# Attention with given scores: the loads of a pass's last two heads moved into a branch, the very last ones in small pieces

## The chip, the cores and the metric

One core of one Trainium2 chip. The metric is the device time of one execution in microseconds (us), the median of several runs.

## The reference

```python
scores: (8, 12, 1024, 1024) float32      v: (8, 12, 1024, 64) float32

def reference(scores, v):
    scores_max = np.max(scores, axis=-1, keepdims=True)
    attn = np.exp(scores - scores_max)
    attn = attn / (np.sum(attn, axis=-1, keepdims=True) + 1e-8)
    return np.matmul(attn, v).astype(np.float32)
```

There are 96 heads (8 x 12). Each has 4 MB of scores, 0.25 MB of v and 0.25 MB of results.

## The kernel before

A loop runs 24 passes of four heads (`AHEAD = 4`). For each head, ScalarE takes the exponential of the scores, two of eight rows at a time (a "row" here is one 128 x 1024 tile), TensorE transposes the tile in eight blocks, VectorE copies the transposed tile from PSUM, and TensorE multiplies it with v, to which a column of ones is joined so that the row sums come out with the product. GpSimd casts v to 16 bits (`vones`) beforehand. The products of a row are emitted two rows later (`LAG = 2`).

```python
    def load(k, n, step=R, **cond):
        queue(nc.sync.dma_start(out=v_bufs[k][:], in_=one(v_bh, n), **cond))
        for r in range(0, R, step):
            queue(nc.sync.dma_start(out=s_bufs[k][:, r : r + step, :],
                                    in_=one(sc_bh, n)[:, r : r + step, :], **cond))

    def load_next(k, n0):
        n = (n0 + (AHEAD + k)) % BH
        load(k, n, R if k < AHEAD - 1 else R // 2, cond=n0 < BH - AHEAD)

    def heads(n0):
        for k in range(AHEAD):
            nc.gpsimd.tensor_copy(out=vones_bufs[k][:, :, 0:D], in_=v_bufs[k][:])
            ...
            for r in range(R):
                if r % EB == 0:
                    p_nat = take(p_bufs)
                    nc.scalar.activation(out=p_nat[:], in_=s_bufs[k][:, r : r + EB, :], func=EXP)
                ...                       # 8 transposes, copy to pt
                if r == R - 1:
                    load_next(k, n0)      # the same buffer, for the next pass
                pending.append((n0 + k, r, pt, st))
                if len(pending) > LAG:
                    finish(pending.pop(0))   # products, division, store of a head
        while pending:
            finish(pending.pop(0))
```

All loads and stores are issued by the sync engine, in order. The framework gives each transfer one of eight completion semaphores in turn; I call them lanes 0 to 7. A transfer's issue waits until the lane's previous user has landed, and whoever reads the data waits for a count on that lane. The packed trace of this kernel has both: the second half of head 95 landed at 1057.22 us and the issue that waited for it began at 1057.35; the scores of head 94 landed at 1046.24 and the exp that waited for them began at 1046.34.

The softmax here doesn't subtract the row's maximum and nothing guards it: scores larger than these inputs give would overflow.

## Time and profile before

| | |
|---|---|
| time | 1071.87 us (1071.53 to 1072.08) |
| span of the profile | 1070.1 us |
| bytes moved | 453.05 MB, at 423 GB/s on average |
| busy: TensorE, ScalarE, VectorE | 70%, 69%, 57% |
| last scores land (read from the sync engine's waits) | about 1057.3 us |
| last exp ends, last result is ready, span ends | 1061.05, 1066.29, 1070.1 us |

Read it from the transfers: their rate is level until the last slice, so the only part of the time that is not transfer is what follows the last byte, some 13 us.

### The profile page before, as it was taken

How to read it: one execution, taken by the hardware profiler on the slowest of the kernel's cores; microseconds unless marked ns; L12 is line 12 of the kernel's file. 1: busy time of each engine (PE TensorE's matmuls, PEld its weight loads, DVE VectorE, ACT ScalarE, POOL GpSimd, SP SyncE). 2: the span in 40 equal slices, each digit the busy share in tenths (PEclk: the TensorE clock that was granted, in tenths of full speed). 3: DMA queues.
4: the chain of work that ended last, by engine and by line, in shares of the span. 5: the costliest groups of instructions: out<-in, count | busy, mean ns of one | idle time of the engine just before them, and what ended most of it. 6: DMA issues, size and time to landing. Idle time of an engine off the chain costs nothing.

```text
span 1070.1 us, 31933 instructions
## 1 busy us (share of the span) xinstructions
PE 752.8 (70%) x12288; PEld 711.3 (66%) x12288; DVE 610.7 (57%) x1157; ACT 733.8 (69%) x408; POOL 60.1 (6%) x102
## 2 busy tenths in 40 slices
PE   3766768677676776677766768668676776767766
PEld 3766767577666676576765758567675676666766
DVE  2655656456565565555655656556564565655655
ACT  4767766677667776676856767677666776576865
POOL 0000000000000000000000000000000000000000
PEclk9888888778897888877887888888897788878889
DMA  9999999999999999999999999999999999999995
GB/s 401 430 410 430 430 431 425 432 436 431 431 426 425 434 427 425 431 431 430 433 427 434 420 442 430 421 433 426 429 426 434 432 431 431 429 424 440 430 420 228
DMA packets 44787, 453.05 MB, mean 423 GB/s; under 512 B 4976, under 2 KB 4976, under 8 KB 29552
## 3 DMA queue, kind: packets, MB, share of 16 engines
q1 hardware_dynamic: 44784, 453.00, 99.7%
q8 instruction: 3, 0.05, 0.0%
HBM read 445.64 MB, written 25.17 MB: 440 GB/s over the span
## 4 chain that ended last, share of the span: by engine, by line
DMA 67%; PEld 9%; PE 9%; DVE 5%; ACT 5%; SPq 2%; issue 2%; ACTq 0%
DMA s_nat<-in_scores_dram 67%; PEld L169 7%; PE psT L169 6%; DVE pt L175 5%; ACT p_nat L163 5%; PE psO L105 3%; PEld L105 3%; SPq L140 1%; SPq L143 1%; SPq L124 0%; DVE recip L116 0%; ACTq L163 0%; DVE out_sb L117 0%
## 5 line engine op out<-in xcount | busy, mean ns | idle before, releaser
L163 ACT ACTIVATE p_nat<-s_nat 128x2048 f16<-128x2048 f32 x384 | 703.0, 1902 | 159.2 <-DMA s_nat<-in_scores_dram 157.0
L175 DVE COPY pt<-psT 128x1024 f16<-128x1024 f16 x768 | 516.3, 690 | 432.3 <-PE L169 214.5
L169 PE MATMUL psT<-ident,p_nat 128*128 128x128 f16 x6144 | 569.7, 251 | 267.3 <-ACT p_nat L163 266.6
L169 PEld LDWEIGHTS <-p_nat 128*128 128x128 f16 x6144 | 492.9, 153 | 282.2 <-ACT p_nat L163 277.7
L105 PE MATMUL psO<-vones,pt 128*128 128x65 f16 x6144 | 374.8, 205 | 45.3 <-DVE pt L175 38.9
L105 PEld LDWEIGHTS <-pt 128*128 128x128 f16 x6144 | 305.2, 106 | 71.8 <-DVE pt L175 70.1
L163 ACT ACT_TABLE_LOAD x24 | 30.8, 1283 | 168.1 <-DMA s_nat<-in_scores_dram 163.2
L158 POOL CAST vones<-v_sb 128x512 f16<-128x512 f32 x96 | 59.4, 619 | 987.6 <-DMA v_sb<-in_v_dram 725.0
L117 DVE TENSOR_TENSOR out_sb<-psO,recip 128x256 f32<-128x256 f32 x192 | 81.1, 422 | 4.9
L116 DVE RECIPROCAL recip<-psO 128x4 f32<-128x4 f32 x192 | 33.5, 174 | 17.2 <-PE psO L105 17.2
L57 DVE MEMSET vones<- 128x8 f16 x4 | 0.2, 65 | 0.8 <-PEq L204 0.8
L51 DVE CAST ident<-ident 128x128 f16<-128x128 f32 x1 | 0.2, 226 | 0.3 <-POOL ident masks.py:199 0.3
masks.py:199 POOL TENSOR_SCALAR_AFFINE_SELECT ident<-ident 128x128 f32<-128x128 f32 x1 | 0.3, 294 | 0.1
masks.py:197 POOL MEMSET ident<- 128x128 f32 x1 | 0.2, 205 | 0.3 <-POOLq L204 0.3
L204 POOL MEMSET const-float32-0.0<- 128x1 f32 x1 | 0.1, 99 | 0.2 <-issue 0.2
L204 POOL MEMSET const-bfloat16-1.0<- 128x1 bf16 x1 | 0.1, 102 | 0.0
L204 POOL MEMSET const-uint8-127<- 128x1 uint8 x1 | 0.1, 102 | 0.0
L204 POOL MEMSET const-float32-1.0<- 128x1 f32 x1 | 0.1, 99 | 0.0
## 6 DMA issues: line engine op xcount, KB each, us to landing
s_nat<-in_scores_dram SPq DMA_DIRECT2D x76, 4096.0 KB, 27.1
s_nat<-in_scores_dram SPq DMA_DIRECT2D x48, 2048.0 KB
v_sb<-in_v_dram SPq DMA_DIRECT2D x100, 256.0 KB, 17.2
out_dram<-out_sb SPq DMA_DIRECT2D x96, 256.0 KB, 21.1
```

What stands on the lines that cost most here:

```text
L51: nc.vector.tensor_copy(out=ident16[:], in_=ident32[:])
L57: nc.vector.memset(vo[:, :, D : D + 1], 1.0)
L105: nc.tensor.matmul(out=psO[:, g, :], lhsT=pt[:, c * P : (c + 1) * P], rhs=st["vones"][:, c, :], start=(c == 0), stop=(c == C - 1),)
L116: nc.vector.reciprocal(out=recip[:], in_=psO[:, :, D : D + 1])
L117: nc.vector.tensor_tensor(out=st["out_sb"][:, r - G + 1 : r + 1, :], in0=psO[:, :, 0:D], in1=recip[:].to_broadcast([P, G, D]), op=mybir.Al ...
L140: queue(nc.sync.dma_start(out=v_bufs[k][:], in_=one(v_bh, n), **cond))
L143: nc.sync.dma_start(out=s_bufs[k][:, r : r + step, :], in_=one(sc_bh, n)[:, r : r + step, :], **cond,)
L158: nc.gpsimd.tensor_copy(out=vones_bufs[k][:, :, 0:D], in_=v_bufs[k][:])
L163: nc.scalar.activation(out=p_nat[:], in_=s_bufs[k][:, r : r + EB, :], func=EXP)
L169: nc.tensor.transpose(out=psT[:, c * P : (c + 1) * P], in_=p_row[:, c, :], identity=ident16[:],)
L175: nc.vector.tensor_copy(out=pt[:], in_=psT[:])
L204: nc = _bacc.Bacc("TRN2", target_bir_lowering=False, num_devices=1)
```

## The change

The intent is to shorten that tail. If the last head arrives in small pieces, ScalarE and TensorE can be nearly done when the last row lands. Small pieces are wanted for the last two heads alone, and in a loop that takes a branch. The branch stands at the end of the pass, so the loads of a pass's heads 2 and 3 (k = 2, 3) are issued after all else of the pass.

```diff
-    def load(k, n, step=R, **cond):
+    def load(k, n, parts=(R,), **cond):
         queue(nc.sync.dma_start(out=v_bufs[k][:], in_=one(v_bh, n), **cond))
-        for r in range(0, R, step):
+        r = 0
+        for rows in parts:
 ...
     def load_next(k, n0):
-        n = (n0 + (AHEAD + k)) % BH
-        load(k, n, R if k < AHEAD - 1 else R // 2, cond=n0 < BH - AHEAD)
+        if k < AHEAD - 2:
+            load(k, (n0 + (AHEAD + k)) % BH, cond=n0 < BH - AHEAD)
+
+    def load_last(n0):
+        ks = range(AHEAD - 2, AHEAD)
+        before = queued[-1:]
+        with tc.If(n0 == BH - 2 * AHEAD) as cmp:
+            queued[:] = before
+            for k, parts in zip(ks, ((4, 4), (2, 2, 2, 1, 1))):
+                load(k, (n0 + (AHEAD + k)) % BH, parts)
+        with cmp.Else():
+            queued[:] = before
+            for k in ks:
+                load(k, (n0 + (AHEAD + k)) % BH, cond=n0 < BH - AHEAD)
 ...
-                    nc.scalar.activation(out=p_nat[:], in_=s_bufs[k][:, r : r + EB, :], func=EXP)
+                    rows = 1 if k == AHEAD - 1 and r == R - EB else EB
+                    for g in range(0, EB, rows):
+                        nc.scalar.activation(out=p_nat[:, g : g + rows, :],
+                                             in_=s_bufs[k][:, r + g : r + g + rows, :], func=EXP)
 ...
         while pending:
             finish(pending.pop(0))
+        load_last(n0)
```

More of the change, by code (lines that the diff above doesn't have):

```diff
@@ L137, in apart @@
         )
-    def load(k, n, step=R, **cond):
+    def load(k, n, parts=(R,), **cond):
         queue(nc.sync.dma_start(out=v_bufs[k][:], in_=one(v_bh, n), **cond))
-        for r in range(0, R, step):
+        r = 0
+        for rows in parts:
             queue(
                 nc.sync.dma_start(
-                    out=s_bufs[k][:, r : r + step, :],
-                    in_=one(sc_bh, n)[:, r : r + step, :],
+                    out=s_bufs[k][:, r : r + rows, :],
+                    in_=one(sc_bh, n)[:, r : r + rows, :],
                     **cond,
@@ L148, in load @@
             )
+            r += rows
     def load_next(k, n0):
-        n = (n0 + (AHEAD + k)) % BH
-        load(k, n, R if k < AHEAD - 1 else R // 2, cond=n0 < BH - AHEAD)
+        if k < AHEAD - 2:
[11 more added lines that the diff above has]
+                load(k, (n0 + (AHEAD + k)) % BH, cond=n0 < BH - AHEAD)
     def heads(n0):
@@ L162, in heads @@
                     p_nat = take(p_bufs)
-                    nc.scalar.activation(
-                        out=p_nat[:], in_=s_bufs[k][:, r : r + EB, :], func=EXP
-                    )
+                    rows = 1 if k == AHEAD - 1 and r == R - EB else EB
+                    for g in range(0, EB, rows):
+                        nc.scalar.activation(
+                            out=p_nat[:, g : g + rows, :],
+                            in_=s_bufs[k][:, r + g : r + g + rows, :],
+                            func=EXP,
+                        )
                 p_row = p_nat[:, r % EB, :].rearrange("p (q c) -> p c q", c=C)
```

## The prediction

> **What bounds the kernel now.** I read the page first, for the load of the DMA queue and the chain that ended last.
>
> ```profile
> GB/s 401 430 410 430 430 431 425 432 436 431 431 426 425 434 427 425 431 431 430 433 427 434 420 442 430 421 433 426 429 426 434 432 431 431 429 424 440 430 420 228
> DMA packets 44787, 453.05 MB, mean 423 GB/s; under 512 B 4976, under 2 KB 4976, under 8 KB 29552
> ...
> DMA 67%; PEld 9%; PE 9%; DVE 5%; ACT 5%; SPq 2%; issue 2%; ACTq 0%
> ```
>
> The transfer rate is flat at about 430 GB/s in all slices but the last: the scores come in as fast as the queue moves them, and no engine is over 70% busy. Only the last slice, 26.75 us, has slack (228 GB/s). So a gain can come only from there, unless the change makes the queue run dry in the middle, which would lose time. Second, the sync engine's timeline over the second-last pass and part of the last.
>
> ```profile
> 1003.12 0.34 SPq L140 DMA_DIRECT2D v_sb<-in_v_dram  x1
> 1004.00 0.33 SPq L143 DMA_DIRECT2D s_nat<-in_scores_dram  x1
> ...
> 1013.43 0.33 SPq L140 DMA_DIRECT2D v_sb<-in_v_dram  x1
> ...
> 1015.75 0.33 SPq L140 DMA_DIRECT2D v_sb<-in_v_dram  x1
> ...
> 1024.48 0.33 SPq L140 DMA_DIRECT2D v_sb<-in_v_dram  x1
> 1025.36 1.19 SPq L143 DMA_DIRECT2D s_nat<-in_scores_dram  x2
> ...
> 1035.43 0.36 SPq L124 DMA_DIRECT2D out_dram<-out_sb  x1
> ...
> 1057.35 0.07 SPq L140 DMA_DIRECT2D v_sb<-in_v_dram  x1
> ```
>
> Each load and store uses one of eight completion semaphores in turn ("lanes" below; the built program's list of waits shows which), and an issue waits until the lane's previous user has landed. So these times are also landing times: 1013.4 is when the last head of a pass has landed (91), 1024.4 head 92, 1035.4 head 93, 1057.3 the second half of head 95. Heads land 11.0 us apart. At 1013.4 one whole load (head 92, issued 1004.0) stands in the queue, and that keeps it full. Third, the tail, by engine.
>
> ```profile
> 983.75 2.88 PE L169 MATMUL psT<-ident,p_nat 128*128 128x128 f16 x24 [6.37 <-ACT p_nat L163]
> ...
> 988.60 0.69 PE L169 MATMUL psT<-ident,p_nat 128*128 128x128 f16 x8
> ...
> 989.38 0.69 PE L169 MATMUL psT<-ident,p_nat 128*128 128x128 f16 x8
> ...
> 1036.68 0.62 POOL L158 CAST vones<-v_sb 128x512 f16<-128x512 f32 x1 [10.36 <-DMA v_sb<-in_v_dram]
> ...
> 1046.34 14.71 ACT L163 ACTIVATE p_nat<-s_nat 128x2048 f16<-128x2048 f32 x8 [3.60 <-DMA s_nat<-in_scores_dram]
> ...
> 1065.87 0.42 DVE L117 TENSOR_TENSOR out_sb<-psO,recip 128x256 f32<-128x256 f32 x1
> 1066.32 0.36 SPq L124 DMA_DIRECT2D out_dram<-out_sb  x1
> ```
>
> GpSimd's cast at 1036.68 is that of v of head 94, whose load stands ahead of that head's scores. The scores of head 94 land whole at 1046.24. ScalarE then runs the eight exps of heads 94 and 95 without a pause to 1061.05, 3.8 us after the last data. The last result is ready at 1066.29, its store goes at 1066.32, the span ends at 1070.1. That tail is what the change aims at.
>
> [...] here 24 transposes take 2.88 us after 6.37 us of idleness (120 ns each) and 8 take 0.69 us later. [...]
>
> **The change part by part.**
>
> Steady state. The loads of the pass's heads 2 and 3 now come after the store of head 3, so after everything else of the pass. Let head 3 land at 0. Its four exps take 7.3 us (8 ran in 14.71), and results come some 5 us after the last exp (1061.05 to 1066.29), so store and branch are reached at about 13. Heads 0 and 1 of the next pass, issued by 0 as before, land at 11 and 22. The queue has some 9 us of work left when head 2's load is issued. The lanes' waits in the normal branch (head 0 landed before head 2's load; head 1 landed, at 22, before the branch is left) leave enough too: head 2's load runs from 22 to 33 with head 3's behind it. No gap: 0 us. The branches [...] and one more exp a pass (about 0.1 us) lie beside transfers: 0 us.
>
> End of the data. The same bytes, except that the store of head 91 now stands ahead of the last loads: 0.26 MB at 430 GB/s is 0.6 us. The last row lands at 1057.3 + 0.6 = 1057.9.
>
> Tail as meant. Half of head 94 lands at about 1042, so ScalarE is no longer behind: the last single-row exp (about 0.97, half of 1.90 and a little) ends at 1058.9.
>
> Tail as built. The two branches use the lanes differently, and one wait must hold for both. In the normal branch lane 0 is first advanced by an empty increment, then by v of head 2: v is the lane's third user of the pass. In the last-heads branch v of head 94 is the second and the last single row of head 95 the third. GpSimd's cast of v for head 2 waits for the full three (the built program's wait value is the pass's last count of this lane). So the cast for head 94, at 1036.68 before, must wait for the very last row: 1057.9 + 0.1, and 0.62 for itself, is 1058.6. TensorE goes in order and lags by two rows: it transposes rows 0, 1 and 2 of head 94, then stands at the first product with v. From 1058.6 it has 13 transposed rows and 16 product rows left, with all exps done. Cold, one row of both takes 1.29 us (transposes started at 1039.31 and 1040.60, at a granted clock of 0.50), warm 0.79 by the starts at 988.60 and 989.38; VectorE needs 0.645 for a copy in a run and (0.17 + 0.42)/4 for the division, 0.80, so I take 0.80. First 3.4 us cold: 2.6 rows. The other 10.4 x 0.80 = 8.3. The last two products behind the copy: 1.2. Sum 1058.6 + 3.4 + 8.3 + 1.2 = 1071.5, and 0.65 for reciprocal and division: 1072.15, against 1066.29: **+5.9 us**.
>
> End. In the last pass the branch's four loads are skipped after the last store, at 0.6 us each (skipped v to skipped s: 1059.29 to 1059.88)[...]. **+0.9 us**. Sum: 1071.84 + 5.9 + 0.9 = **1078.6 us**.
>
> **The rivals.** (a) The tail as meant, the wait on the lane being looser than I read it: from the last exp at 1058.9, transposes 0.6, copy 0.7, products 0.45, reciprocal and division 0.65: 1061.3, so -5.0, and +0.9: 1067.7 us. For it speaks the change's intent; against it the wait value, which is the same register value in every pass and has to be right for the normal branch. (b) The queue runs dry once a pass, because heads 2 and 3 are asked for a head later: against it 9 us of queued work; if head 3's compute took 23 instead of 13 us, it would lose a microsecond or more in each of 23 passes, 1100 us or more. [...] (c) The wait stands, but TensorE with a full backlog keeps the pace of ScalarE-fed pairs in the tail before, 1.93 us for two rows: 10.4 x 0.165 = 1.7 us more, 1080.3. (d) [...] the cold stretch is a second window long: 1 to 2 us more.
>
> **Range and chances.** The spread of (c) and (d) above the value[...] make 1074.5 to 1083. Reading (a) has 7%, (b) 4%. The 2% limits are 1050.4 and 1093.3: neither tail reaches them; only (b) passes the upper. Faster 0.01, same 0.95, slower 0.04.
>
> **What would show it.** GpSimd's second-last cast (v of head 94) starting beside the last one, near 1058, after a wait of some 30 us, would show the lane; so would TensorE idle from about 1046 to 1058 and then 13 us of solid work, with ScalarE done by 1059. Rates of 430 GB/s in the slices before, and landings 11.0 us apart, would show the steady state untouched. Stores of the last pass all after 1058. I am wrong if that cast starts near 1037, or if slices in the middle fall under 420 throughout.

Passages of the recorded text that no trace of this case showed are cut where marked, and with them terms of its sum. For the end it had 3.3 us behind the last result, against 2.4 before, hence the +0.9.

Two of its figures can be read from traces. The first is the 3.4 us that TensorE runs cold, at a granted clock of 0.50. In the trace before, the clock is 0.50 from 1038.51 to 1041.92 and from 1048.75 to 1052.16, 3.41 us each, and for 3.56 us from the first of the 24 transposes at 983.75. But the packed trace has longer stretches as well: of 58 at half clock, 25 last 3.41 us, 24 last 6.83 and 9 last 10.24. So the "second window" of rival (d) is to be read as one more 3.4 us at half clock, worth 1.3 us by the figures of the prediction (3.4 less 2.6 rows of 0.80); its "1 to 2" is an estimate. The second is the exp more in a pass: in the trace after, five exps take 7.41 us (at 1013.56) where four take 7.33, so 0.08 us.

## The result, and the profile after

| | before | after |
|---|---|---|
| time, median | 1071.87 us | 1082.47 us (1082.28 to 1082.69) |
| ratio | | 1.0099 (95% interval 1.0082 to 1.0117) |
| span of the profile | 1070.1 us | 1080.7 us |

A ratio here and below is the mean time of one kernel's runs over the mean of the other's in the same rounds, so not quite the ratio of the medians. The change costs 10.6 us.

First the page of the changed kernel: the rates of 40 slices (27.0 us each now), and the totals.

```profile
GB/s 397 426 427 425 430 432 435 424 425 435 428 434 427 437 427 431 427 431 430 432 427 423 433 428 438 425 437 427 437 422 433 432 428 428 423 436 425 441 415 53
DMA packets 42195, 453.05 MB, mean 419 GB/s; under 512 B 4688, under 2 KB 4688, under 8 KB 29520
...
DMA 4%; issue 1%; PEld 1%; PE 1%; DVE 1%; SPq 0%; ACT 0%; DVEq 0%; ACTq 0%
```

The rate in the middle is what it was; the last slice falls from 228 to 53 GB/s. The same bytes move at the same pace, and afterwards there is more time in which nothing moves. The chain of waits, which led back to the start before, 67% of it transfers, now covers only what follows 982.5 us, and it books TensorE's standstill in the tail as 11.0 us of "issue", which is to say without a cause. So the timelines have to tell it. Next the sync engine's timeline over the second-last pass and the start of the last (columns: start, length, line, operation; x3 merges three issues with the waits between them).

```profile
1003.26 0.33 SPq L144 DMA_DIRECT2D s_nat<-in_scores_dram  x1
...
1013.51 0.33 SPq L140 DMA_DIRECT2D v_sb<-in_v_dram  x1
...
1014.95 11.10 SPq L124 DMA_DIRECT2D out_dram<-out_sb  x3
1026.55 0.35 SPq L140 DMA_DIRECT2D v_sb<-in_v_dram  x1
1027.26 1.22 SPq L144 DMA_DIRECT2D s_nat<-in_scores_dram  x2
...
1034.83 3.20 SPq L144 DMA_DIRECT2D s_nat<-in_scores_dram  x5
1057.57 0.10 SPq L140 DMA_DIRECT2D v_sb<-in_v_dram  x1
```

Head 91 has landed at 1013.5 as before. The branch is entered at 1026.5, 13 us later; the five pieces of head 95 follow when head 93 has landed (1034.8, before 1035.4). The skipped load at 1057.57 waits for the last row: the data end at 1057.5, against 1057.3 before. Now the tail by engine.

```profile
1057.59 1.18 POOL L173 CAST vones<-v_sb 128x512 f16<-128x512 f32 x2 [31.82 <-DMA s_nat<-in_scores_dram]
```

```profile
1042.29 3.71 ACT L180 ACTIVATE p_nat<-s_nat 128x2048 f16<-128x2048 f32 x2 [0.16 <-DMA s_nat<-in_scores_dram]
...
1055.07 3.80 ACT L180 ACTIVATE p_nat<-s_nat 128x2048 f16<-128x2048 f32 x3 [0.54 <-DMA s_nat<-in_scores_dram]
```

```profile
1046.58 0.42 PE L105 MATMUL psO<-vones,pt 128*128 128x65 f16 x8
1058.26 0.55 PE L105 MATMUL psO<-vones,pt 128*128 128x65 f16 x7 [11.26 <-POOL vones L173]
...
1065.61 0.68 PE L188 MATMUL psT<-ident,p_nat 128*128 128x128 f16 x8
...
1071.57 0.68 PE L188 MATMUL psT<-ident,p_nat 128*128 128x128 f16 x8
```

```profile
1074.44 0.42 DVE L117 TENSOR_TENSOR out_sb<-psO,recip 128x256 f32<-128x256 f32 x1
1074.89 0.33 SPq L124 DMA_DIRECT2D out_dram<-out_sb  x1
1076.19 0.10 SPq L140 DMA_DIRECT2D v_sb<-in_v_dram  x1
...
1077.77 0.07 SPq L144 DMA_DIRECT2D s_nat<-in_scores_dram  x1
```

The casts of v of heads 94 and 95 run together at 1057.59, and the bracket says what ended GpSimd's 31.82 us of idleness: a transfer of *scores*. A cast of v has no use for scores. The one for head 94 ran at 1036.68 before. ScalarE does what the change intended: it starts head 94 at 1042.29 instead of 1046.34 and ends at 1058.87, 1.4 us after the last byte. But TensorE stands still for 11.3 us for the cast, and all the rest of heads 94 and 95 comes after it. The clock and the busy time in the two stretches that follow:

```profile
1058.00:1064.00 6.00, 5.75 (x74) 5.74 (x74) 2.86 (x5) 0.87 (x1) 0.76 (x2) 0.50 0.23 87
1064.00:1075.00 11.00, 8.89 (x169) 8.15 (x167) 8.45 (x17) 0.00 (x0) 0.00 (x0) 1.00 0.06 24
```

The columns are the stretch, its length, busy time of PE, PEld, DVE, ACT and POOL, then TensorE's granted clock, the share of the transfer engines and GB/s. TensorE is busy almost throughout the first 6 us, but at half clock.

### The profile page after: what moved, and what is told of

The parts are those of the page before. It is cut to its first block, busy times and chain, and to the rows that moved or that the text cites. A ratio compares the mean times of both kernels' runs of the same rounds, so it can differ in the third digit from the quotient of the medians.

```text
span 1080.7 us, 32380 instructions
## 1 busy us (share of the span) xinstructions
PE 765.6 (71%) x12288; PEld 726.4 (67%) x12288; DVE 610.0 (56%) x1157; ACT 736.2 (68%) x432; POOL 59.8 (6%) x102
## 5 line engine op out<-in xcount | busy, mean ns | idle before, releaser
L180 ACT ACTIVATE p_nat<-s_nat 128x2048 f16<-128x2048 f32 (+1 forms) x408 | 705.4, 1800 | 253.0 <-DMA s_nat<-in_scores_dram 130.6
L188 PE MATMUL psT<-ident,p_nat 128*128 128x128 f16 x6144 | 586.7, 255 | 256.2 <-ACT p_nat L180 255.4
L188 PEld LDWEIGHTS <-p_nat 128*128 128x128 f16 x6144 | 503.6, 154 | 273.7 <-ACT p_nat L180 270.3
L105 PEld LDWEIGHTS <-pt 128*128 128x128 f16 x6144 | 310.9, 107 | 73.7 <-DVE pt L194 59.2
```

Of the source, the lines that this page charges most:

```text
L105: nc.tensor.matmul(out=psO[:, g, :], lhsT=pt[:, c * P : (c + 1) * P], rhs=st["vones"][:, c, :], start=(c == 0), stop=(c == C - 1),)
L180: nc.scalar.activation(out=p_nat[:, g : g + rows, :], in_=s_bufs[k][:, r + g : r + g + rows, :], func=EXP,)
L188: nc.tensor.transpose(out=psT[:, c * P : (c + 1) * P], in_=p_row[:, c, :], identity=ident16[:],)
```

## The experiments

The theory: in both arms of the branch, transfers use the lanes in turn, but nine in one arm and four in the other, so the normal arm is filled up with empty increments (additions to a semaphore without a transfer, so that both arms leave it at the same count). On lane 0 the pass's first user is v of head 0; then come the increment and v of head 2 in the normal arm, but v of head 94 and the last row of head 95 in the other. One wait value serves both, and it is the later one. The packed trace of the changed kernel bears this out, in records that the views of `prof` do not print. In the normal arm the sync engine adds to lane 0's semaphore at 982.48 and then issues v of head 2 on it at 982.96. In the other arm v of head 94 lands on lane 0 at 1037.32 and the last row on the same lane at 1057.44; GpSimd's wait on that semaphore ends at 1057.46. The rival: the branch, the late issue or the small pieces cost the time by themselves. Each experiment was run in three rounds. The fifth answers what the third left open.

**1. Eight transfers instead of nine.** The last head in four pieces, so that no lane is used twice in the arm.

```diff
-            for k, parts in zip(ks, ((4, 4), (2, 2, 2, 1, 1))):
+            for k, parts in zip(ks, ((4, 4), (2, 2, 2, 2))):
```

> The changed kernel with the last head in pieces of 2,2,2,2 rows, so that the last-heads branch issues eight transfers and none shares its completion lane with v of head 94. Lane theory: GpSimd's cast of v of head 94 starts near 1037 instead of 1057.6, TensorE does not idle for 11 us, the last result comes near 1062 instead of 1074.9; the end after it stays at 5.8 us; 1069.5 to 1071 us. Rival (small pieces, the branch or the late issue cost the time): the time stays within 2 us of 1082.5.

Measured: 1070.14 us (1069.93 to 1070.41), ratio 0.9984 to the kernel before. GpSimd's timeline of this run:

```profile
1037.60 0.62 POOL L173 CAST vones<-v_sb 128x512 f16<-128x512 f32 x1 [11.80 <-PE L105]
1047.92 0.62 POOL L173 CAST vones<-v_sb 128x512 f16<-128x512 f32 x1 [9.70 <-PE psO L105]
```

The two casts are apart again, at 1037.60 and 1047.92; the last result is ready at 1062.58. The branch, the late issue and pieces are all still there, so none of them makes the 12 us. This edit changes the pieces as well, though.

**2. The branch with whole heads in both arms.**

```diff
-            for k, parts in zip(ks, ((4, 4), (2, 2, 2, 1, 1))):
+            for k, parts in zip(ks, ((R,), (R,))):
```

> The branch with whole heads in both arms: late issue and branch alone, no pieces, no ninth transfer. Lane theory: head 95 lands whole at about 1057.4, its four exps end at 1064.9, the last result near 1067.8, and 5.4 us to the end: 1074 to 1076 us. Rival (branch and late issue cost the time by themselves): 1080 us or more, with transfer rates below 425 GB/s in the middle.

Measured: 1076.21 us (1075.23 to 1076.67), ratio 1.0041. The last head lands whole, and the tail follows from there (timelines of ScalarE and VectorE):

```profile
1057.25 7.42 ACT L180 ACTIVATE p_nat<-s_nat 128x2048 f16<-128x2048 f32 x5 [2.95 <-DMA s_nat<-in_scores_dram]
```

```profile
1067.93 0.42 DVE L117 TENSOR_TENSOR out_sb<-psO,recip 128x256 f32<-128x256 f32 x1
```

Five exps from 1057.25 to 1064.67, the last result at 1068.35. With both arms alike no wait is stretched: 6 us better than the change, though its last head comes in one piece. The time is 0.2 us above my range, and far below the rival's. Against the run of eight pieces it shows what pieces are worth over whole heads: 1076.21 - 1070.14 = 6.1 us. (The kernel before had the last head in two halves, so the gain over it is smaller.)

**3. Both loads of v ahead of the branch.** All nine transfers and all pieces stay.

```diff
+        for k in ks:
+            load_v(k, (n0 + (AHEAD + k)) % BH, cond=n0 < BH - AHEAD)
         before = queued[-1:]
         with tc.If(n0 == BH - 2 * AHEAD) as cmp:
 ...
-                load(k, (n0 + (AHEAD + k)) % BH, parts)
+                load_s(k, (n0 + (AHEAD + k)) % BH, parts)      # scores alone; so in the other arm
```

> The changed kernel with the same pieces 4,4 and 2,2,2,1,1, but with the two loads of v ahead of the branch, so that v of head 94 is the second user of its lane in both arms while the last row stays the third. Lane theory: the cast waits for v alone, the last result near 1061.5, 1068.5 to 1070.5 us. Rival (the ninth transfer or the single-row pieces are slow in themselves): the time stays near 1082.

Measured: 1073.65 us (1073.06 to 1075.95), ratio 1.0022. The big loss is gone, but I had expected 3 us less. The edit moved the lanes of the scores, and ScalarE's timeline shows a new stretched wait, in the normal arm this time:

```profile
1006.32 3.71 ACT L188 ACTIVATE p_nat<-s_nat 128x2048 f16<-128x2048 f32 x2 [5.63 <-DMA s_nat<-in_scores_dram]
1016.00 11.02 ACT L188 ACTIVATE p_nat<-s_nat 128x2048 f16<-128x2048 f32 x7 [5.97 <-DMA s_nat<-in_scores_dram]
```

Head 2 of this pass gets two exps and then stands 5.97 us until head 3 has landed, although its own scores arrived whole. The built program's waits say why: lane 3 carries the second half of head 94 in one arm and all scores of head 3 in the other, and the third exp waits for it. (The packed trace agrees: ScalarE's wait on lane 3 ends at 1015.92, when that lane's transfer lands at 1015.90.) The store that stands before the branch is late by that, which is how I explain that the passes are longer; no run tests it: from the third pass's first exps to the last pass's it takes 924.6 us, against 922.0 in run 5. That is 2.6 of the 3.5 us between the two.

**4. The pass's last store behind the branch**, on top of the eight pieces.

```diff
+        load_last(n0)
         while pending:
             finish(pending.pop(0))
-        load_last(n0)
```

> As the run with eight pieces, and the branch emitted before the pass's last results, so that the store of its last head stands behind the branch. If the branch on the sync engine's way to the end costs the extra 2 us after the last result: the end after the last result falls from 5.8 to about 3.8 us, 1067.5 to 1069 us. If the end is longer for another reason, it stays at 5.8 us and the time equals the run with eight pieces.

Measured: 1068.86 us (1068.69 to 1069.27), ratio 0.9972 (0.9956 to 0.9989). VectorE's last result and the sync engine's last store of this run:

```profile
1062.03 0.42 DVE L117 TENSOR_TENSOR out_sb<-psO,recip 128x256 f32<-128x256 f32 x1
1063.03 0.36 SPq L124 DMA_DIRECT2D out_dram<-out_sb  x1
```

The result is ready at 1062.45, as in run 1 (1062.58), and the span ends at 1066.9, 4.45 us later instead of 5.6. The store itself is 0.58 us late, because the sync engine is still in the branch (the last skipped load is over at 1062.17, the empty increments follow); from the store on it takes 3.9 us, as the kernel before did. So the branch's work at the very end is worth 1.3 us. This is the fastest kernel.

**5. One load moved: v of head 2 ahead of the branch.** It keeps its place in the queue, its lane and everything else; only its order against the empty increment of the normal arm changes.

```diff
+        load_v(ks[0], (n0 + (AHEAD + ks[0])) % BH, cond=n0 < BH - AHEAD)
         before = queued[-1:]
         with tc.If(n0 == BH - 2 * AHEAD) as cmp:
 ...
-                load(k, (n0 + (AHEAD + k)) % BH, parts)
+                load(k, (n0 + (AHEAD + k)) % BH, parts, with_v=k != ks[0])    # so in the other arm
```

> The changed kernel with one load moved: v of the pass's head 2 stands ahead of the branch, in the same place of the queue and on the same lane, so it comes before the empty increment of the normal arm. Nine transfers, pieces, single rows and lanes of all others stay. Lane theory: the cast of v of head 94 starts near 1037, all the loss goes: the last result near 1061.5 to 1062.5, 5.8 us to the end, 1069 to 1070.5 us. Rival (what the earlier run with both v ahead lost, or the nine pieces themselves): 1073 us or more.

Measured: 1070.13 us (1069.85 to 1070.82), ratio 0.9985. GpSimd's and VectorE's timelines:

```profile
1037.65 0.62 POOL L178 CAST vones<-v_sb 128x512 f16<-128x512 f32 x1 [11.78 <-PE L105]
```

```profile
1062.12 0.42 DVE L117 TENSOR_TENSOR out_sb<-psO,recip 128x256 f32<-128x256 f32 x1
```

The cast of head 94 is back at 1037.65 and the last result at 1062.54, 12.3 us before that of the changed kernel, with the same nine pieces on the same lanes. The packed trace has both landings on lane 0 as before, v of head 94 at 1037.50 and the last row at 1057.61, and the empty increment of the normal arm now after the loads. This settles it: the loss is the one wait that had to cover two orders. The time equals that of run 1, so single-row pieces gain nothing over pieces of two rows: ScalarE ends at 1059.04, and TensorE and VectorE are the last here.

**6. Ten transfers.** A dose more: the last head in six pieces.

```diff
-            for k, parts in zip(ks, ((4, 4), (2, 2, 2, 1, 1))):
+            for k, parts in zip(ks, ((4, 4), (2, 2, 1, 1, 1, 1))):
```

> The changed kernel with the last head in 2,2,1,1,1,1 rows: ten transfers in the arm, so lane 1 (scores of head 94, first half) is shared with the last row and lane 0 (v of head 94) with the last but one. Lane theory: ScalarE does not start head 94 at 1042.3 but only when the last row has landed, near 1057.5; nine exps, 14.9 us, end near 1072.5; TensorE follows ScalarE and the last result comes near 1076; 5.9 us to the end: 1083 to 1085 us. Rival (single-row pieces help, ten are as good as nine): 1081 to 1082.5, ScalarE starting at 1042.

Measured: 1085.88 us (1085.23 to 1086.02), ratio 1.0132. ScalarE's timeline:

```profile
1034.75 7.32 ACT L180 ACTIVATE p_nat<-s_nat 128x2048 f16<-128x2048 f32 x4 [2.42 <-DMA s_nat<-in_scores_dram]
1057.63 14.63 ACT L180 ACTIVATE p_nat<-s_nat 128x2048 f16<-128x2048 f32 x9 [15.55 <-DMA s_nat<-in_scores_dram]
```

With the tenth transfer on lane 1, which head 94's first half uses, ScalarE too stands still, 15.55 us, until the last row has landed, and then runs all nine exps of two heads in one go. The theory foretold the start and the length; the last result came at 1077.45 where I had said 1076, and the time is 0.9 us above my range.

**7. No branch.** Sixteen transfers in every pass, pieces always, the last store behind them.

```diff
-        with tc.If(n0 == BH - 2 * AHEAD) as cmp:
-            ...
-        with cmp.Else():
-            ...
+        for k, parts in zip(ks, ((4, 4), (2, 2, 2, 2))):
+            load(k, (n0 + (AHEAD + k)) % BH, parts, cond=n0 < BH - AHEAD)
```

> No branch: the last two heads of every pass in pieces 4,4 and 2,2,2,2 (16 transfers a pass, so each lane is used twice a pass and no wait covers two arms), last store behind the loads. If branches cost something beside the end: below the 1068.9 us of the run with eight pieces and the store last, at 1067 to 1068.5 us. If pieces in all passes slow the transfers [...], the rate falls and the time rises above 1070.

Measured: 1071.66 us (1071.61 to 1072.01), ratio 0.9998. The second of the two came true: the tail is short, but the data end later. From the third pass's first exps to the last pass's it takes 925.4 us for 21 passes, 44.07 each, against 922.1, 43.91 each, in the changed kernel. A pass takes 0.16 us more, 3.3 us in all, which is about what the tail gains. That the small pieces are the cause is not shown: the edit also takes the branch away and puts sixteen transfers a pass on the eight lanes, whose waits hold back the issues. So this run shows that the branch pays, and not why.

**8. The kernel before with single-row exps alone.**

```diff
-                    nc.scalar.activation(out=p_nat[:], in_=s_bufs[k][:, r : r + EB, :], func=EXP)
+                    rows = 1 if k == AHEAD - 1 and r == R - EB else EB
+                    for g in range(0, EB, rows):
+                        nc.scalar.activation(...)      # as in the change
```

> The kernel before with only the single-row exps of the last head of a pass. Both theories: these exps cost about 0.1 us a pass beside transfers and can bring a row's transposes forward by 0.9 us at the very end, where TensorE is 1.5 us behind ScalarE anyway: 1071.3 to 1072.3 us, the same as before.

Measured: 1071.61 us (1071.52 to 1072.32), ratio 1.0000. The last nine exps take 14.79 us (at 1046.06), where eight took 14.71 before. This part of the change costs nothing and gains nothing by itself.

## Why the prediction was right, and which terms were off

The time on record was 1078.6 us with a range of 1074.5 to 1083; measured were 1082.5, near the upper end. "Within 2%" was right.

- **Steady state, 0 us: right.** The branch was entered 13.0 us after head 3 had landed, as worked out, with 8.2 us of queued work left (head 93 landed at 1034.8; predicted were some 9). The compare-and-branch of the sync engine took 0.06 to 0.13 us in the packed trace, 0.12 on average. 21 passes took 922.1 us against 922.6 before.
- **End of the data: 0.4 us off.** The store of head 91 was to delay the last row to 1057.9; it landed at 1057.5. The passes were a little quicker, and the 0.6 us was lost in that.
- **The lane: right.** The cast was to start at 1058.0 and did at 1057.59. Runs 5 and 6 show the cause, one by taking away the false wait with all nine transfers kept, the other by adding a second.
- **TensorE's work behind it: 12.9 us predicted, 1058.6 to 1071.5; 15.7 measured, 1058.26 to 1073.97.** Three terms were too small. "First 3.4 us cold" was 5.7: the granted clock is 0.50 from 1050.32, within TensorE's 11.3 us of idleness, to 1063.97, and six rows took 7.0 us (starts of transposes at 1058.61 and 1065.61), 0.9 more than by my figures. "13 transposed rows" were 14: the scheduler had put the first product of head 94 ahead of the transposes of its third row, so only two rows were done when TensorE stopped. I had counted from the source and not from the list of instructions. "I take 0.80" for a warm row was 0.85 (seven intervals from 1065.61 to 1071.57), perhaps because many transposes come in pairs and VectorE's copies with them, which no run tests. These make 0.9, 0.8 and 0.4 us of the 2.8; the rest lies in 0.35 us before the first transpose and 1.55 instead of 1.2 us behind the last row. Rival (d), the longer cold stretch, was true, and rival (c), the slower pace, in part: its figure was 0.965 a row.
- **The end: +0.9 us predicted, +2.0 measured.** From the last result to the end of the span it was 1070.1 - 1066.29 = 3.8 us and became 1080.7 - 1074.86 = 5.8. The skipped loads were right: the last is over at 1077.84, 2.95 us after the store was issued. The four increments and the leaving of the loop then took 2.9 us, 1.1 more than I had. The packed trace divides them: the increments are over at 1078.40, some 0.6 us, and leaving the loop takes the other 2.3. Before, the last store landed at 1068.32, 1.64 us after its issue was over, so what followed it was 1.8 us; and the first steps of leaving (1066.72 to 1067.17) lay beside its landing. After the branch nothing hides them, since the store has landed at 1076.92, before the skipped loads are over. Run 4 shows that 1.3 us goes when the store stands behind the branch.
- **Sum.** +8.6 for the last result and +2.0 for the end make the 10.6 us; I had +5.9 and +0.9.
- **The tail as meant, rival (a), 1067.7:** false for the change, and too good even without the false wait: run 5 gives 1070.13, since the last result comes at 1062.54, not at 1061.3, and the end is 1.1 us longer than I took.
- **The range held partly by luck.** Of the 3.9 us between 1078.6 and 1082.5, the slower pace and the longer cold stretch, which the range was made for, are 1.3. The fourteenth row (0.8) and the longer end (1.1) were not among its reasons, and 0.5 us more would have left it. In rival (b), a microsecond in each of 23 passes makes 1095 us, not 1100.

The expected gain itself, then, is small, out of a tail of 13: 1.7 us with eight pieces, where the interval of the ratio (0.9967 to 1.0000) ends at no change, and 3.0 us with the store moved, which is clear of noise.

## What to carry to other kernels

Where transfers share completion semaphores and the two arms of a branch issue different numbers of them, write down for each semaphore which transfer is its first, second and third user in each arm: in the runs here a reader of one of them waited for the later place of the two (the cast until 1057.46, though its v had landed at 1037.32). Moving a load that both arms need ahead of the branch cured it in run 5, and keeping the arm to eight transfers in run 1, but neither is a rule: run 3 has two loads ahead and arms of seven and two transfers, and there another wait was stretched by 5.97 us. Only the list for each semaphore decides. Then look in the profile for a wait that was ended by a tensor that the waiting instruction does not read: that is the mark of it. Such a wait need not cost anything. In run 1 GpSimd's cast for head 91 starts at 1013.55, when that head's scores have landed, though its v landed at 1003.73 (in run 2, with equal arms, it starts at 1003.70); but 21 passes take 922.0 us there and 921.9 in run 2.
